# Input projection of a two-layer hybrid encoder: the last K pair of a chunk pair multiplied column by column, one more weight tile fed, heads turned in reversed order

## The chip, the cores and the metric

One NeuronCore of a Trainium2 chip. The metric is the device time of one execution of the whole program in microseconds, the median of several runs. Engine names in what follows: TensorE (PE in the profile, PEld its weight loads), VectorE (DVE), ScalarE (ACT), GpSimd (POOL), SyncE (SP), which issues nearly all transfers.

## The reference

Two layers over 256 tokens of width 2048, all in float32. Each layer mixes the tokens with 16 heads and then applies a gated feed-forward part:

```python
h = rms_norm(x, pre_mix_norm[l])
proj = h @ w_in                  # 6144 columns: q, k, v of 8 stick-breaking heads, then of 8 differential heads
o_sb = rms_norm(stick_breaking_attention(q_sb, k_sb, v_sb), sb_out_norm)
o_d  = rms_norm(differential_attention(q1, q2, k1, k2, v_d, lam), diff_subln) * (1.0 - lam_init)
x = x + rms_norm(concat(o_sb, o_d) @ w_o, post_mix_norm[l])
h = rms_norm(x, pre_ffn_norm[l])
x = x + rms_norm((silu(h @ w_gate) * (h @ w_up)) @ w_down, post_ffn_norm[l])
```

The stick-breaking heads weigh each earlier key by a sigmoid and by the cumulative product of what the keys between have left over; the differential heads subtract two softmaxes and rotate a quarter of each query and key (partial rotary).

## The kernel before, in words

**Float32 by halves.** Every operand of a big matmul is split into a rounded half `hi` and a remainder `lo`, and a product of two such operands takes three matmuls: hi by hi (L1254 in the input projection), lo of the weights (L1255), lo of the activations (L1256). The activations stand still in TensorE (128 by 128), and 512 weight columns stream past them.

**The weight stream.** All weights lie in DRAM in the order of use, which `weight_order` writes out (L119 and L120 for the plain part of the input projection), as tiles of 512 KB: 128 partitions, two K blocks, 512 columns. SyncE loads each into one of four `raw` buffers (L285), ScalarE rounds it to `hi` (L407 plain; L355, L362, L381 for mixed tiles), and VectorE subtracts to get `lo` (L346). `hi` and `lo` have six buffers each, handed round in the order of the tiles. When TensorE's program asks for a tile with `weights(i, ahead)`, the jobs of the tiles up to `ahead` further on are written into the program of ScalarE and VectorE; LOOKAHEAD = 4 (L29). A scheduler then orders each engine's instructions, and each engine works through its own list in that order.

**The input projection.** The 6144 columns are 12 chunks of 512, taken in six pairs, PAIRS = ((6, 8), (10, 7), (9, 0), (11, 2), (1, 3), (4, 5)). Chunks 0 to 5 are q, k and v of the stick-breaking heads, 6 to 11 those of the differential heads; even ones hold heads 0 to 3, odd ones heads 4 to 7. A chunk pair has four PSUM banks: two token tiles t by two columns (`col` 0 or 1). K is worked off in eight K pairs `kp`. In all but the first chunk pair some of the K pairs come first in a form of seven products in place of eight (`phased`; their tiles are mixed ones, with a `u1` tile for the parts that stay); the rest are plain (`eight_in`, L1050). In the last plain K pair `eight_in` runs for t = 0 alone, with both columns, and `settle(0)` evicts the two banks, then the same for t = 1. `settle` (L1080) copies each bank by ScalarE into a token tile `tok` (L1095) or into v (L1089), and has GpSimd rotate the differential q and k. The very first chunk pair is in `opening` (L966), without feeding ahead.

**Attention between the matmuls.** `tick()` is called throughout, and lets waiting generators issue a step. `flip` (L1099) turns a chunk's four heads by TensorE (L1113) and ScalarE (L1114); when q and k of a group are there, `stick_weights` or `diff_weights` makes the attention weights, and `attend` (L810) multiplies them with v for two heads at a time, into a bank `o` of which there is one. `attending` lets one head pair hold it; `norm_pair` (L766) takes squares (L774), scales by VectorE into `on` (L779), and lowers `attending` (L782); some ticks later TensorE turns the result into `oT_ps` (L795), and ScalarE and VectorE make the two halves of `mix` (L797, L800), which is the stationary operand of the output projection.

**The output projection** runs mixed for the K pairs 4 to 6 and plain for 7, 0, 2, 1, 3. K pair 1 needs the head pair `sb0_0_1`, its tiles are 110 and 111; K pair 3 needs the last head pair of all, `sb0_1_1`, its tiles are 112 and 113. Tiles 114 and 115 belong to the next columns and to heads that are long done; 116 and 117 are loaded into buffers V (L285) and mixed with each other (L328, L322), and before these loads stand reloads of `x` (L479) on SyncE. In layer 1 the same tiles carry numbers higher by 394, and the stage lies 1078 us later.

Of the kernel before, what the change touches and what calls it, by code (L numbers as in the profile page):

```python
# [9 lines left out]
F32 = mybir.dt.float32  # L10
F32R = mybir.dt.float32r
BF16 = mybir.dt.bfloat16
AF = mybir.ActivationFunctionType
# [4 lines left out]
P = 128  # L18
# [3 lines left out]
NT = S // P  # L22
KT = D // P
NH = 8
FF = 5632
CW = 512
# [62 lines left out]
def weight_order():  # L89
# [7 lines left out]
    def queue_pair(name, l, kp, c):  # L97
        return queue((name, l, 2 * kp, c), (name, l, 2 * kp + 1, c))
# [14 lines left out]
    for l in range(L):  # L113
        lay = {"in": {}, "o": {}, "gate": {}, "up": {}, "down": {}}
        for n, (ca, cb) in enumerate(PAIRS):
            if n:
                queue_phase(("in", l, n), "w_in", l, IN_SEVENS[n], (ca, cb))
            for kp in IN_PLAIN[n]:
                lay["in"][ca, kp] = queue_pair("w_in", l, kp, ca)  # L119
                lay["in"][cb, kp] = queue_pair("w_in", l, kp, cb)  # L120
        queue_phase(("o", l), "w_o", l, O_PHASED, (0, 1))
        order_o = [(c, kp) for kp in O_PLAIN for c in (0, 1)]
        order_o += [(c, kp) for kp in LATE_O for c in (2, 3)] + [(c, kp) for c in (2, 3) for kp in LAST_O]
# [71 lines left out]
def kernel(  # L195
# [262 lines left out]
    def weights(i, ahead):  # L458
        feed_jobs(jobs_to[i] + ahead)
        return ready[i]  # L460
# [309 lines left out]
    def norm_pair(pool, ob, mix, mixed, h0, gcol, nm):  # L770
        ss = small.tile([P, 4], F32, tag="oss", name=f"oss_{nm}")
        for i in range(4):
# [6 lines left out]
        nc.vector.tensor_tensor(  # L779
            out=on, in0=ob.rearrange("p (i d) -> p i d", i=4), in1=rs.unsqueeze(2).to_broadcast([P, 4, P]), op=ALU.mult  # L780
        )
        attending[0] -= 1  # L782
        yield
        yield
        if nm[0] == "d":
            yield
# [179 lines left out]
    def opening(pool, accs, xT, stats, sums_of, settle):  # L966
# [47 lines left out]
        for kp in range(KT // 2):  # L1014
            if kp:
                split(2 * kp)
                split(2 * kp + 1)
            if kp + 2 < KT // 2:
                load()
                fetch(2 * kp + 6)  # L1020
            for part in ((0,), (1,)) if kp == KT // 2 - 1 else (range(NT),):
                eight_in(accs, xT, 0, PAIRS[0], kp, part, kp == 0, kp == KT // 2 - 1, 0)
                if kp == KT // 2 - 1:
                    settle(part[0])
            if 3 <= kp < 7:
                next(stats)
            if 3 <= kp < 5:
                sums_of(kp - 3)
# [21 lines left out]
    def eight_in(accs, xT, l, cc, kp, toks, first, last, ahead=LOOKAHEAD):  # L1050
        ws = [weights(plan[l]["in"][c, kp], ahead) for c in cc]
        for kk in range(2):
            for t in toks:
                tick()
                st = xT[2 * kp + kk]
                stat = (st[:, 0, t * P : (t + 1) * P], st[:, 1, t * P : (t + 1) * P])
                for col, (hi, lo) in enumerate(ws):
                    product(accs[2 * t + col], stat, (hi[:, kk, :], lo[:, kk, :]), first and kk == 0, last and kk == 1)
# [8 lines left out]
    def mixer_in(pool, l, rs, xT, mix, mixed, began):  # L1067
# [7 lines left out]
        for n, cc in enumerate(PAIRS):  # L1075
# [1 line left out]
            alone = n == len(PAIRS) - 1  # L1077
            toks = {}

            def settle(t):  # L1080
                with tc.high_priority(offset=URGENT):
                    for col, c in enumerate(cc):
                        kind, g = divmod(c, 2)
                        src = banks[2 * t + col]
                        st = heads.setdefault((kind // 3, g), {"w": {}, "pT": {}, "scored": 0})
                        if kind in (2, 5):
                            if t == 0:
                                st["half"] = pool.tile([P, NT, CW], F32, tag="v", bufs=2, name=f"v{l}_{c}")
                            nc.scalar.activation(st["half"][:, t, :], src, AF.Copy, scale=rs[t][:, 0:1])  # L1089
                            if t == 1:  # L1090
                                st["v"] = st["half"]
                            continue
                        by = {0: 1, 1: 0, 3: 2, 4: 0}[kind]
                        tok = pool.tile([P, CW], F32, tag="tok", name=f"tok{l}_{c}_{t}")
                        nc.scalar.activation(tok, src, AF.Copy, scale=rs[t][:, by : by + 1])  # L1095
                        if kind in (3, 4):
                            rotate(pool, tok, t, f"{l}_{c}_{t}")
                        toks[c, t] = tok

            def flip(c, toks):  # L1100
                kind, g = divmod(c, 2)
# [27 lines left out]
            else:  # L1129
# [6 lines left out]
                for j, kp in enumerate(kps):  # L1136
# [12 lines left out]
                        rs += [inv_rms(t, pool, f"in{l}", part=began[1][t]) for t in range(NT)]  # L1149
                        scales(rs)  # L1150
                    if last:
                        for t in range(NT):
                            eight_in(banks, xT, l, cc, kp, (t,), False, last)
                            settle(t)
                    else:
                        eight_in(banks, xT, l, cc, kp, range(NT), False, last)
# [94 lines left out]
    def product(a, stat, moving, first, last):  # L1251
        sh, sl = stat
        hi, lo = moving
        nc.tensor.matmul(a, sh, hi, start=first, stop=False, skip_group_check=open_sums[0])  # L1254
        nc.tensor.matmul(a, sh, lo, start=False, stop=False, skip_group_check=open_sums[0])  # L1255
        return nc.tensor.matmul(a, sl, hi, start=False, stop=last, skip_group_check=open_sums[0])  # L1256
# [526 lines left out]
```

## Time and profile before

| | |
|---|---|
| median of 3 runs | 2170.24 us (2170.0 to 2171.7) |
| the profiled execution | 2169.97 us, its span 2168.3 us |
| TensorE busy | 2154.1 us, 99% of the span |
| VectorE, ScalarE, GpSimd busy | 1986.9, 1434.7, 241.1 us |
| input projection, layer 0 / layer 1 | up to about 299 us / 1078 to 1377 us |
| TensorE clock granted | 0.999 of full speed |

Reading it: a row of a timeline gives the start in us from the span's beginning, the duration in us, engine, line, operation, output <- inputs by the program's names, shapes and types, a count when like instructions follow one another, and in brackets how long the engine stood idle before it and for whom. A row of the windows gives the stretch, its length, busy time and count of instructions for PE, PEld, DVE, ACT and POOL, then the granted clock, the share of the DMA engines and GB/s. A row of the waits gives the engine, what it waited for, the sum in us, how often, and the longest.

### The profile page before, as it was taken

The numbers are of one execution on the slowest core, as the hardware profiler recorded it, in microseconds if no ns is written. First come the engines' busy times: TensorE is split into PE (matmuls) and PEld (weight loads), VectorE is DVE, ScalarE is ACT, GpSimd is POOL, SyncE is SP. The second block draws the span as 40 slices with busy tenths as digits, with TensorE's granted clock in tenths as the row PEclk, the third lists the DMA queues.
The fourth block names the chain that finished last, engine by engine and source line by source line (L and its number), as shares of the span: only waits on it lengthen the run. The fifth ranks groups of instructions, "written<-read, shape, count | busy, mean of one in ns | idle before, by whom it ended". The sixth has DMA issues, their size and how long they took to land.

```text
span 2168.3 us, 28898 instructions
## 1 busy us (share of the span) xinstructions
PE 2154.1 (99%) x9896; PEld 1773.9 (82%) x9896; DVE 1986.9 (92%) x2767; ACT 1434.7 (66%) x2163; POOL 241.1 (11%) x234
## 2 busy tenths in 40 slices
PE   9999999999999999999999999999999999999998
PEld 7888888888888888888878888888888888888887
DVE  7898987899999999999897989888999999999997
ACT  7667775766766666666575777757566666666664
POOL 1110000021221220000020100000112222100000
PEclk9999999999999999999999999999999999999999
DMA  8554556497887776777465555555978878767683
GB/s 295 183 193 157 173 175 246 156 309 235 243 264 224 233 240 226 227 228 253 147 207 188 176 182 175 182 204 190 308 218 269 242 224 241 230 218 245 201 270 99
DMA packets 143155, 470.43 MB, mean 217 GB/s; under 512 B 16272, under 2 KB 17296, under 8 KB 142496
## 3 DMA queue, kind: packets, MB, share of 16 engines
q1 hardware_dynamic: 124832, 436.03, 57.9%
q0 software_dynamic: 17600, 32.02, 9.0%
q8 instruction: 77, 1.26, 0.2%
q14 instruction: 70, 0.57, 0.1%
q10 hardware_dynamic: 576, 0.54, 0.1%
HBM read 460.14 MB, written 8.39 MB: 216 GB/s over the span
## 4 chain that ended last, share of the span: by engine, by line
PE 91%; DVE 4%; ACT 2%; DMA 2%; issue 1%; DVEq 0%; ACTq 0%
PE c L1311 21%; PE in L1255 5%; PE in L1254 5%; PE in L1256 5%; PE dn L1634 4%; PE dn L1631 4%; PE dn L1632 4%; PE p L1255 3%; PE p L1256 3%; PE c L1255 3%; PE c L1254 3%; PE c L1256 3%; PE p L1254 3%; DVE lo L346 2%; PE o L693 2%; PE o L695 2%
## 5 line engine op out<-in xcount | busy, mean ns | idle before, releaser
L346 DVE TENSOR_TENSOR lo<-raw,hi 128x1024 fp32r<-128x1024 f32 (+1 forms) x512 | 594.6, 1179 | 62.1 <-ACT hi L407 35.8
L407 ACT ACTIVATE hi<-raw 128x1024 fp32r<-128x1024 f32 x440 | 450.9, 1057 | 107.2 <-DMA raw<-in_weights_in_turn_dram 71.9
L1311 PE MATMUL c<-hi,xF 128*128 128x512 f32 x1344 | 364.3, 392 | 0.5 <-DVE xF L608 0.5
L1311 PEld LDWEIGHTS c<-hi,xF 128*128 128x128 f32 x1344 | 249.9, 188 | 52.6 <-DVE xF L608 1.3
L301 POOL DMA_DIRECT2D T<-in_weights_in_turn_dram x122 | 106.9, 876 | 1364.8 <-DMA T<-in_weights_in_turn_dram 279.2
L1311 PE MATMUL c<-lo,xF 128*128 128x512 f32 x672 | 207.5, 390 | 0.0
L322 ACT ACTIVATE Th<-T 128x512 fp32r<-128x512 f32 x122 | 77.2, 632 | 182.8 <-DVE T L333 180.6
L322 ACT ACTIVATE Th<-G 128x1024 fp32r<-128x1024 f32 x122 | 129.0, 1058 | 77.0 <-DVE G L334 75.8
L1631 PE MATMUL dn<-hi,jh 128*128 128x512 f32 x416 | 162.1, 390 | 0.0
L1632 PE MATMUL dn<-lo,jh 128*128 128x512 f32 x416 | 161.9, 389 | 0.0
L324 DVE TENSOR_TENSOR Tl<-G,Th 128x1024 fp32r<-128x1024 f32 x122 | 148.8, 1220 | 11.6 <-ACT Th L322 11.6
L407 ACT ACTIVATE hi<-G 128x1024 fp32r<-128x1024 f32 x122 | 129.0, 1057 | 41.6 <-DMA G<-in_weights_in_turn_dram 21.3
L324 DVE TENSOR_TENSOR lo<-T,hi 128x1024 fp32r<-128x1024 f32 x122 | 152.1, 1247 | 0.0
L334 DVE TENSOR_TENSOR G<-G,T 128x1024 f32<-128x1024 f32 x122 | 148.6, 1218 | 1.8
L1311 PEld LDWEIGHTS c<-lo,xF 128*128 128x128 f32 x672 | 126.0, 188 | 26.4
L346 DVE TENSOR_TENSOR lo<-G,hi 128x1024 fp32r<-128x1024 f32 x106 | 129.2, 1219 | 10.5 <-ACT hi L407 10.5
L322 ACT ACTIVATE hi<-T 128x1024 fp32r<-128x1024 f32 x122 | 128.1, 1050 | 12.0 <-PE c L1256 9.1
L1634 PE MATMUL dn<-hi,jl 128*128 128x512 f32 x416 | 128.2, 389 | 0.0
L1254 PE MATMUL in<-hi,xT 128*128 128x512 f32 x309 | 122.2, 398 | 0.8 <-ACT hi L1008 0.8
L1255 PE MATMUL in<-lo,xT 128*128 128x512 f32 x309 | 120.9, 392 | 1.4 <-DVE lo L346 1.4
L1256 PE MATMUL in<-hi,xT 128*128 128x512 f32 x309 | 120.3, 390 | 0.0
L1254 PE MATMUL in<-hi,xI 128*128 128x512 f32 x285 | 114.2, 401 | 0.0
(462 smaller groups left out, 5064.3 us busy)
## 6 DMA issues: line engine op xcount, KB each, us to landing
raw<-in_weights_in_turn_dram SPq DMA_DIRECT2D x510, 512.0 KB, 4.9
T<-in_weights_in_turn_dram SPq DMA_DIRECT2D x122, 512.0 KB, 5.3
G<-in_weights_in_turn_dram SPq DMA_DIRECT2D x122, 512.0 KB, 5.4
T<-in_weights_in_turn_dram POOLq DMA_DIRECT2D x122, 256.0 KB, 5.6
u<-in_weights_in_turn_dram SPq DMA_DIRECT2D x36, 256.0 KB, 5.7
V<-in_weights_in_turn_dram SPq DMA_DIRECT2D x8, 512.0 KB, 4.6
away_ffn<-x SPq DMA_DIRECT2D x8, 512.0 KB, 7.2
xd<-away_ffn SPq DMA_DIRECT2D x8, 512.0 KB, 8.7
```

What stands on the lines that cost most here:

```text
L322: nc.scalar.activation(h, w, AF.Copy)
L324: newest_rest[i] = nc.vector.tensor_tensor(out=l, in0=w, in1=h.bitcast(F32), op=ALU.subtract)
L334: nc.vector.tensor_tensor(out=g, in0=g, in1=t2.unsqueeze(1).to_broadcast([P, 2, CW]), op=ALU.add)
L346: rests.append(nc.vector.tensor_tensor(out=lo, in0=src, in1=hi.bitcast(F32), op=ALU.subtract))
L407: nc.scalar.activation(hi, raw, AF.Copy)
L1254: nc.tensor.matmul(a, sh, hi, start=first, stop=False, skip_group_check=open_sums[0])
L1255: nc.tensor.matmul(a, sh, lo, start=False, stop=False, skip_group_check=open_sums[0])
L1256: return nc.tensor.matmul(a, sl, hi, start=False, stop=last, skip_group_check=open_sums[0])
L1311: nc.tensor.matmul(a, stat[part], w[j][:, kk, :], start=first and kk + n == 0, stop=last and kk == 1 and n == 2)
L1631: nc.tensor.matmul(accs[c, t], sh, hi[:, kk, :], start=first, stop=False, skip_group_check=open_sums[0])
L1632: nc.tensor.matmul(accs[c, t], sh, lo[:, kk, :], start=False, stop=False, skip_group_check=open_sums[0])
L1634: nc.tensor.matmul(accs[c, t], sl, hi[:, kk, :], start=False, stop=last, skip_group_check=open_sums[0])
```

## The change

Four edits, all in the order of the work; the instructions of every engine stay the same in kind and number.

1. In the last plain K pair of a chunk pair, the weight stream has the tile of column 1 ahead of that of column 0.
2. The new `last_in` works that K pair column by column: column 1 for both token tiles, then column 0; after each token tile `settle(t, col)` evicts one bank. Before column 1 the stream is fed four tiles ahead, before column 0 five; in `opening` too, where nothing was fed ahead before.
3. The chunks of a pair start to be turned in reversed order, the second first.
4. `norm_pair` lowers `attending` one step later, so that a head pair holds the bank `o` for one step (two ticks) more.

```diff
@@ -116,8 +116,8 @@
             for kp in IN_PLAIN[n]:
-                lay["in"][ca, kp] = queue_pair("w_in", l, kp, ca)
-                lay["in"][cb, kp] = queue_pair("w_in", l, kp, cb)
+                for c in (cb, ca) if kp == IN_PLAIN[n][-1] else (ca, cb):
+                    lay["in"][c, kp] = queue_pair("w_in", l, kp, c)
...
@@ -779,8 +779,8 @@
+        yield
         attending[0] -= 1
-        yield
         yield
...
@@ -1018,10 +1018,10 @@
-            for part in ((0,), (1,)) if kp == KT // 2 - 1 else (range(NT),):
-                eight_in(accs, xT, 0, PAIRS[0], kp, part, kp == 0, kp == KT // 2 - 1, 0)
-                if kp == KT // 2 - 1:
-                    settle(part[0])
+            if kp == KT // 2 - 1:
+                last_in(accs, xT, 0, PAIRS[0], kp, settle)
+            else:
+                eight_in(accs, xT, 0, PAIRS[0], kp, kp == 0, 0)
...
@@ -1047,15 +1047,30 @@
+    def last_in(accs, xT, l, cc, kp, settle):
+
+        newest = plan[l]["in"][cc[0], kp]
+        ws = [weights(plan[l]["in"][c, kp], 0) for c in cc[::-1]][::-1]
+        for col in (1, 0):
+            feed_jobs(jobs_to[newest] + LOOKAHEAD + 1 - col)
+            hi, lo = ws[col]
+            for t in range(NT):
+                tick()
+                for kk in range(2):
+                    st = xT[2 * kp + kk]
+                    stat = (st[:, 0, t * P : (t + 1) * P], st[:, 1, t * P : (t + 1) * P])
+                    product(accs[2 * t + col], stat, (hi[:, kk, :], lo[:, kk, :]), False, kk == 1)
+                settle(t, col)
...
@@ -1077,25 +1092,25 @@
-            def settle(t):
+            def settle(t, col):
+                c = cc[col]
...
@@ -1149,11 +1164,9 @@
                     if last:
-                        for t in range(NT):
-                            eight_in(banks, xT, l, cc, kp, (t,), False, last)
-                            settle(t)
+                        last_in(banks, xT, l, cc, kp, settle)
...
@@ -1161,7 +1174,7 @@
             wait = 3
-            for c in cc:
+            for c in cc[::-1]:
```

(`eight_in` loses its arguments `toks` and `last`, and the rest of `settle` is unindented.)

ScalarE's program at the start of the sixth chunk pair in layer 0, before. `hi83` and `hi85` are rounded tiles of the sixth pair, `tok0_1_0` is layer 0, chunk 1, token tile 0; `a_sb` are the weights of a stick-breaking head pair in the making.

```order
L362 ACTIVATE hi83_1_2387<-raw83_2379 128x512
L1095 ACTIVATE tok0_1_0_2424<-in0_1_0_1950,rs_in0_0_494 128x512
L1095 ACTIVATE tok0_3_0_2426<-in0_3_0_1951,rs_in0_0_494 128x512
L855 ACTIVATE a_sb0_0_1_2414<-zb_sb0_0_1_2407 128x256
L797 ACTIVATE mix_df0_1_0_2428<-oT_ps_df0_1_0_2429,gains_89 128x256
L856 ACTIVATE a_sb0_0_1_2414<-a_sb0_0_1_2414 128x768
L797 ACTIVATE mix_df0_1_0_2428<-oT_ps_df0_1_0_2429,gains_89 128x256
L858 ACTIVATE a_sb0_0_1_2414<-a_sb0_0_1_2414 128x768
L1095 ACTIVATE tok0_1_1_2453<-in0_1_1_1952,rs_in0_1_508 128x512
L1095 ACTIVATE tok0_3_1_2455<-in0_3_1_1953,rs_in0_1_508 128x512
L355 ACTIVATE hi85_0_2468<-raw85_2466 128x1024
L362 ACTIVATE hi85_1_2474<-u1_84_0_2462 128x512
```

And after:

```order
L1110 ACTIVATE tok0_3_0_2398<-in0_3_0_1952,rs_in0_0_494 128x512
L918 ACTIVATE e1_df0_1_2_1_2389,sm_df0_1_2_1_2387<-s1_df0_1_2_1_2340,mx_df0_1_2_1_2345 128x256
L1110 ACTIVATE tok0_3_1_2408<-in0_3_1_1954,rs_in0_1_508 128x512
L362 ACTIVATE hi83_1_2380<-raw83_2372 128x512
L355 ACTIVATE hi85_0_2416<-raw85_2414 128x1024
L1110 ACTIVATE tok0_1_0_2428<-in0_1_0_1951,rs_in0_0_494 128x512
L1110 ACTIVATE tok0_1_1_2440<-in0_1_1_1953,rs_in0_1_508 128x512
L362 ACTIVATE hi85_1_2447<-u1_84_0_2410 128x512
L855 ACTIVATE a_sb0_0_1_2464<-za_sb0_0_1_2456 128x512
L362 ACTIVATE hi85_1_2447<-raw85_2414 128x512
L855 ACTIVATE a_sb0_0_1_2464<-zb_sb0_0_1_2457 128x256
L856 ACTIVATE a_sb0_0_1_2464<-a_sb0_0_1_2464 128x768
```

The tile `hi85_0` stood behind all four evictions and the steps of `a_sb`; now it follows `hi83_1` and the two evictions of chunk 3, with chunk 1's evictions and `a_sb` behind it.

TensorE's program in the output projection of layer 0, before; `o0_c_t` are the banks, `oT_ps_sb0_1_1` the last head pair turned.

```order
L694 MATMUL o0_1_1_2952<-lo109_3225,mix_sb0_1_0_1_3238 128x512
L695 MATMUL o0_1_1_2952<-hi109_3224,mix_sb0_1_0_1_3238 128x512
L795 MATMUL oT_ps_sb0_1_1_3387<-ident_90,on_sb0_1_1_3347 128x128 x4
L693 MATMUL o0_0_0_2949<-hi110_3262,mix_sb0_0_1_0_3328 128x512
L694 MATMUL o0_0_0_2949<-lo110_3263,mix_sb0_0_1_0_3328 128x512
L695 MATMUL o0_0_0_2949<-hi110_3262,mix_sb0_0_1_0_3328 128x512
L693 MATMUL o0_0_1_2951<-hi110_3262,mix_sb0_0_1_0_3328 128x512
```

And after:

```order
L693 MATMUL o0_1_1_2950<-hi111_3280,mix_sb0_0_1_1_3338 128x512
L694 MATMUL o0_1_1_2950<-lo111_3281,mix_sb0_0_1_1_3338 128x512
L695 MATMUL o0_1_1_2950<-hi111_3280,mix_sb0_0_1_1_3338 128x512
L795 MATMUL oT_ps_sb0_1_1_3417<-ident_90,on_sb0_1_1_3383 128x128 x4
L693 MATMUL o0_2_0_3485<-hi114_3371,mix_df0_1_0_2482 128x512
L694 MATMUL o0_2_0_3485<-lo114_3372,mix_df0_1_0_2482 128x512
L695 MATMUL o0_2_0_3485<-hi114_3371,mix_df0_1_0_2482 128x512
L693 MATMUL o0_2_1_3487<-hi114_3371,mix_df0_1_0_2482 128x512
L694 MATMUL o0_2_1_3487<-lo114_3372,mix_df0_1_0_2482 128x512
L695 MATMUL o0_2_1_3487<-hi114_3371,mix_df0_1_0_2482 128x512
L693 MATMUL o0_0_0_2947<-hi112_3308,mix_sb0_1_1_0_3415 128x512
L694 MATMUL o0_0_0_2947<-lo112_3309,mix_sb0_1_1_0_3415 128x512
```

The turning of `sb0_1_1` stood ahead of tile 110's matmuls; it now follows those of tile 111, 24 matmuls later, and six matmuls of tile 114 stand between it and the first matmul that uses `mix_sb0_1_1_0`.

ScalarE's program in the same place, before:

```order
L407 ACTIVATE hi112_3324<-raw112_3322 128x1024
L407 ACTIVATE hi113_3363<-raw113_3361 128x1024
L797 ACTIVATE mix_sb0_1_1_0_3385<-oT_ps_sb0_1_1_3387,gains_89 128x256
L407 ACTIVATE hi114_3381<-raw114_3379 128x1024
L797 ACTIVATE mix_sb0_1_1_1_3386<-oT_ps_sb0_1_1_3387,gains_89 128x256
L407 ACTIVATE hi115_3410<-raw115_3408 128x1024
L407 ACTIVATE hi116_3428<-V116_3426 128x1024
L322 ACTIVATE hi117_3452<-V117_3450 128x1024
L700 ACTIVATE jm_o0_0_0_3444,ssm_o0_0_2947<-o0_0_0_2949 128x512
```

And after:

```order
L407 ACTIVATE hi113_3333<-raw113_3331 128x1024
L576 ACTIVATE ors_sb0_1_1_3375<-rsq_sb0_1_1_3376 128x4
L797 ACTIVATE mix_sb0_0_1_1_3338<-oT_ps_sb0_0_1_3339,gains_89 128x256
L407 ACTIVATE hi114_3371<-raw114_3369 128x1024
L407 ACTIVATE hi115_3399<-raw115_3397 128x1024
L407 ACTIVATE hi116_3428<-V116_3426 128x1024
L322 ACTIVATE hi117_3452<-V117_3450 128x1024
L797 ACTIVATE mix_sb0_1_1_0_3415<-oT_ps_sb0_1_1_3417,gains_89 128x256
L797 ACTIVATE mix_sb0_1_1_1_3416<-oT_ps_sb0_1_1_3417,gains_89 128x256
L322 ACTIVATE T2h117_3456<-V117_3450 128x512
L700 ACTIVATE jm_o0_0_0_3444,ssm_o0_0_2945<-o0_0_0_2947 128x512
```

The copies `mix_sb0_1_1_0` and `_1` stood around `hi114`; they now stand behind `hi116` and `hi117`, the tiles that are made from V. Layer 1 shows the same two shifts.

More of the change, by code (lines that the diff above doesn't have):

```diff
@@ L1048, in scales, with eight_in @@
             nc.vector.tensor_scalar_mul(rs[t][:, 2:3], rs[t][:, 0:1], 1.0 / 8.0)
-    def eight_in(accs, xT, l, cc, kp, toks, first, last, ahead=LOOKAHEAD):
+    def eight_in(accs, xT, l, cc, kp, first, ahead=LOOKAHEAD):
         ws = [weights(plan[l]["in"][c, kp], ahead) for c in cc]
         for kk in range(2):
-            for t in toks:
+            for t in range(NT):
                 tick()
@@ L1057, in eight_in @@
                 for col, (hi, lo) in enumerate(ws):
-                    product(accs[2 * t + col], stat, (hi[:, kk, :], lo[:, kk, :]), first and kk == 0, last and kk == 1)
+                    product(accs[2 * t + col], stat, (hi[:, kk, :], lo[:, kk, :]), first and kk == 0, False)
+    def last_in(accs, xT, l, cc, kp, settle):
[4 more added lines that the diff above has]
+            hi, lo = ws[col]
+            for t in range(NT):
+                tick()
[4 more added lines that the diff above has]
+                settle(t, col)
     def pair_forms(pool, spool, bufs, tiles, kp, nm, **kw):
@@ L1078, in mixer_in @@
             toks = {}
-            def settle(t):
-                with tc.high_priority(offset=URGENT):
[L1082 to L1098, printed above, removed]
+            def settle(t, col):
+                c = cc[col]
+                kind, g = divmod(c, 2)
+                src = banks[2 * t + col]
+                st = heads.setdefault((kind // 3, g), {"w": {}, "pT": {}, "scored": 0})
+                with tc.high_priority(offset=URGENT):
+                    if kind in (2, 5):
+                        if t == 0:
+                            st["half"] = pool.tile([P, NT, CW], F32, tag="v", bufs=2, name=f"v{l}_{c}")
+                        nc.scalar.activation(st["half"][:, t, :], src, AF.Copy, scale=rs[t][:, 0:1])
+                        if t == 1:
+                            st["v"] = st["half"]
+                        return
+                    by = {0: 1, 1: 0, 3: 2, 4: 0}[kind]
+                    tok = pool.tile([P, CW], F32, tag="tok", name=f"tok{l}_{c}_{t}")
+                    nc.scalar.activation(tok, src, AF.Copy, scale=rs[t][:, by : by + 1])
+                    if kind in (3, 4):
+                        rotate(pool, tok, t, f"{l}_{c}_{t}")
+                    toks[c, t] = tok
             def flip(c, toks):
@@ L1151, in mixer_in @@
                     if last:
-                        for t in range(NT):
-                            eight_in(banks, xT, l, cc, kp, (t,), False, last)
-                            settle(t)
+                        last_in(banks, xT, l, cc, kp, settle)
                     else:
-                        eight_in(banks, xT, l, cc, kp, range(NT), False, last)
+                        eight_in(banks, xT, l, cc, kp, False)
                     if ahead and heads[0, 1].keys() >= {"qdone", "kdone"}:
```

## The prediction

> **What bounds the kernel now.** I began with the page: busy time per engine and the chain that ended last.
>
> ```profile
> span 2168.3 us, 28898 instructions
> PE 2154.1 (99%) x9896; PEld 1773.9 (82%) x9896; DVE 1986.9 (92%) x2767; ACT 1434.7 (66%) x2163; POOL 241.1 (11%) x234
> PE 91%; DVE 4%; ACT 2%; DMA 2%; issue 1%; DVEq 0%; ACTq 0%
> ```
>
> TensorE is the bound, busy 2154.1 of 2168.3 us, and the change takes no matmul away and adds none. So the end moves only with TensorE's waits, and these I read next, from its waits by releaser.
>
> ```profile
> PE in L1255 <- DVE lo L346: 4.0, 8, 0.7
> ```
>
> Eight times, 4.0 us in all, the second matmul of a product (L1255, on the low half `lo` of a weight tile) waits for VectorE's subtraction (L346) that makes that half. This is what the change can remove. TensorE's timeline shows where; six of the eight waits lie in two places per layer: where the sixth chunk pair begins (252 and 255 us, in layer 1 at 1330 and 1333), and where the fourth does (154 and 1233).
>
> ```profile
> 250.93 0.39 PE L1256 MATMUL in<-hi,xT 128*128 128x512 f32 x1
> 251.16 0.40 PE L1254 MATMUL in<-hi,xT 128*128 128x512 f32 x1
> 252.30 0.50 PE L1255 MATMUL in<-lo,xT 128*128 128x512 f32 x1 [0.74 <-DVE lo L346]
> ...
> 254.98 0.50 PE L1255 MATMUL in<-lo,shin 128*128 128x512 f32 x1 [0.56 <-DVE lo L346]
> ...
> 1330.38 0.50 PE L1255 MATMUL in<-lo,xI 128*128 128x512 f32 x1 [0.38 <-DVE lo L346]
> ...
> 1333.05 0.50 PE L1255 MATMUL in<-lo,shin 128*128 128x512 f32 x1 [0.56 <-DVE lo L346]
> ...
> 154.23 0.50 PE L1255 MATMUL in<-lo,shin 128*128 128x512 f32 x1 [0.55 <-DVE lo L346]
> ...
> 1232.75 0.50 PE L1255 MATMUL in<-lo,shin 128*128 128x512 f32 x1 [0.54 <-DVE lo L346]
> ```
>
> Undisturbed matmuls start 0.23 us apart (250.93 to 251.16). The waiting one starts 1.14 after its forerunner (251.16 to 252.30): 0.91 lost, of which the bracket shows 0.74. The other 0.17 is TensorE's pipeline filling again, so every such wait costs its bracket and 0.17: 0.91 + 0.73 in layer 0 and 0.55 + 0.73 in layer 1 at the sixth pair, 2.92 us; 0.72 + 0.71 at the fourth, 1.43 us.
>
> Why is `lo` late at the sixth pair? VectorE's timeline there, then ScalarE's.
>
> ```profile
> 244.76 0.48 DVE L800 SCALAR_TENSOR_TENSOR mix_df<-oT_ps_df,gains,mix_df 128x256 fp32r<-128x256 f32 x1 [0.69 <-ACT mix_df L797]
> 245.85 0.48 DVE L800 SCALAR_TENSOR_TENSOR mix_df<-oT_ps_df,gains,mix_df 128x256 fp32r<-128x256 f32 x1 [0.61 <-ACT mix_df L797]
> 246.58 0.69 DVE L860 SCALAR_TENSOR_TENSOR a_sb<-za_sb,a_sb 128x512 f32<-128x512 f32 x1 [0.25 <-ACT a_sb L858]
> ...
> 248.69 1.22 DVE L346 TENSOR_TENSOR lo<-raw,hi 128x1024 fp32r<-128x1024 f32 x1 [1.08 <-ACT hi L355]
> ```
>
> ```profile
> 242.30 0.63 ACT L362 ACTIVATE hi<-raw 128x512 fp32r<-128x512 f32 x1 [1.63 <-DVE raw L360]
> ...
> 246.42 1.29 ACT L1095 ACTIVATE tok<-in,rs_in 128x512 f32<-128x512 f32 x2
> 247.56 1.09 ACT L355 ACTIVATE hi<-raw 128x1024 fp32r<-128x1024 f32 x1
> ```
>
> VectorE stands idle 0.69 + 0.61 + 0.25 + 1.08 = 2.63 us in front of the late subtractions, and the last of these waits is for `hi` (L355, tile 85), which ScalarE makes at 247.56, behind two evictions (L1095) that need the end of the fifth pair. The weights themselves are long there.
>
> ```profile
> 224.80 35.15 SPq L285 DMA_DIRECT2D raw<-in_weights_in_turn_dram  x8
> ```
>
> The group's first two loads (224.80 and the next) are tiles 85 and 86, over 20 us before their use: a queue order and a feeding limit, not a transfer, hold them.
>
> **The change part by part.** *Column by column, and a fifth tile fed.* In ScalarE's new order `hi85_0` stands right behind the second half of `hi83_1`, the row at 242.30, and no longer behind the exponentials and all four evictions. Its buffer is that of tile 79 (six rotate), and 79 is now used up by the first half of the last plain pair. So it can start near 242.9 instead of 247.56, and VectorE's 2.63 us of idle time can fill. The two waits need `lo` 0.91 + 0.73 = 1.64 us earlier, counting that TensorE itself comes earlier after the first; 2.63 covers that with 1.0 to spare, and layer 1 asks for less (1.28). Bounds: nothing gained, if `hi86` (its buffer is tile 82's, first used by the sixth pair itself) holds the second `lo`; all 2.92 at best. I take **-2.92**, because the buffer of 82_0 is free after that pair's first six matmuls, which is before `lo` of 86 is wanted. At the fourth pair it is another matter:
>
> ```profile
> 138.00:154.00 16.00, 15.68 (x73) 12.42 (x71) 15.81 (x30) 12.96 (x26) 7.24 (x8) 1.00 0.20 71
> ```
>
> VectorE (the third of the busy times) works 15.81 of the 16 us before that wait. An earlier `hi` does little for an engine without idle time; I take 0 there, and -1.43 as the bound. The two waits left of the eight, 0.67 of brackets (4.0 less the 3.33 of the six rows), lie at the start and in the second pair; I take 0 for them too. Evicting by column costs nothing: no row of TensorE's waits names an eviction (L1095, L1089), and the four are as many as before. On SyncE the two `u` loads of the sixth pair (`u1_81`) go ahead of five loads of 512 KB:
>
> ```profile
> raw<-in_weights_in_turn_dram SPq DMA_DIRECT2D x510, 512.0 KB, 4.9
> ```
>
> The 20 us of lead above cover that; without it a tile would land late by up to these 4.9 us. GpSimd, 11% busy, turns the heads of column 8 before those of column 6, two jobs of one length.
>
> *Heads turned in reversed order, a pair attending one tick longer.* No row of the waits names the bank `o`, so the longer hold by itself is worth 0. But both push the last stick-breaking head pair, `sb0_1_1`, back, and this meets the output projection, where order decides. In the new order TensorE's transposes of that pair (L795) come 24 matmuls later, six matmuls ahead of the first use of their result, and ScalarE copies the result (L797) behind `hi116` and `hi117`, which are made from V, the last loads of the queue. Before:
>
> ```profile
> 342.91 1.06 ACT L407 ACTIVATE hi<-V 128x1024 fp32r<-128x1024 f32 x1 [1.55 <-DMA V<-in_weights_in_turn_dram]
> 346.00 1.06 ACT L322 ACTIVATE hi<-V 128x1024 fp32r<-128x1024 f32 x1 [2.03 <-DVE V L328]
> 346.96 0.58 ACT L700 ACTIVATE jm_o<-o 128x512 f32<-128x512 f32 x1
> ```
>
> ```profile
> 336.17 0.47 ACT L797 ACTIVATE mix_sb<-oT_ps_sb,gains 128x256 fp32r<-128x256 f32 x1
> ```
>
> ```profile
> 341.44 0.39 PE L693 MATMUL o<-hi,mix_sb 128*128 128x512 f32 x1
> ...
> 342.80 0.39 PE L693 MATMUL o<-hi,mix_sb 128*128 128x512 f32 x1
> ```
>
> The copy was made at 336.17 and first used at 341.44. Now six matmuls of `hi114` stand in between, so TensorE wants it at 342.80; ScalarE is free of `hi117` at 346.96 and takes 0.47: 347.43. By these times TensorE would wait 4.6 us; queued behind the copy on ScalarE are the second copy and the squares (L700), and behind the waiting matmul all of TensorE. In layer 1 V comes sooner:
>
> ```profile
> 1420.87 0.39 PE L693 MATMUL o<-hi,mix_sb 128*128 128x512 f32 x1
> ```
> ```profile
> 1422.12 0.58 ACT L700 ACTIVATE jm_o<-o 128x512 f32<-128x512 f32 x1
> ```
>
> There it is 1422.12 + 0.47 - 1420.87 = 1.7 us. These are upper ends, since V may land earlier. Its load follows the `x` reloads on SyncE, which wait for VectorE, and the transfers have nothing to do before them:
>
> ```profile
> 314.42 2.69 SPq L479 DMA_DIRECT2D x<-in_x_dram  x4
> ```
> ```profile
> 310.00:314.00 4.00, 4.00 (x21) 3.41 (x22) 4.00 (x6) 2.34 (x3) 0.00 (x0) 1.00 0.01 2
> ```
> ```profile
> 299.04 1.23 DVE L346 TENSOR_TENSOR lo<-raw,hi 128x1024 fp32r<-128x1024 f32 x1 [2.60 <-ACT hi L355]
> ...
> 1377.11 1.23 DVE L346 TENSOR_TENSOR lo<-raw,hi 128x1024 fp32r<-128x1024 f32 x1 [2.93 <-ACT hi L355]
> ```
>
> DMA share 0.01 from 310 to 314. VectorE stood idle 2.60 us (2.93) at the end of the sixth pair, again for a `hi` behind evictions, which the fifth tile moves ahead of them; from there to the reloads it has no gap. If that fills, the reloads, and V behind them, come as much sooner against TensorE: 4.6 - 2.6 = 2.0 us left in layer 0, 1.7 - 2.9 below zero, so 0, in layer 1. The ends are 0 and 6.3 for both; I take **+2.0**, the reading of the rows just quoted.
>
> Sum: -2.92 + 2.0 = -0.9 against the profiled execution (2169.97 us: span 2168.3 and 1.7 around it), 2169.1. The median of the runs, 2170.24, is 0.27 above it; by the median I say **2169.3 us**. About 0.2% of it, 4.3 us, is what a measurement can tell from no change.
>
> **The rivals.** *Faster:* V lands early enough that the output projection has no wait, and the waits at the fourth pair go too, since the tile order there moves as well: -2.92 - 1.43 = -4.35, 2165.9 us. For it speaks the empty DMA stretch, against it VectorE's 15.81 of 16 us.
>
> *Slower:* the copies wait for V as before's times have it, because VectorE spends the freed 2.6 us on other queued work and the reloads start no sooner against TensorE; and only the first wait in each layer's sixth pair goes (0.91 + 0.55 = 1.46). Then 4.6 + 1.7 - 1.46 = +4.8, 2175.1 us. V's `hi` decides it: if both layers come d sooner, the loss is 4.6 + 1.7 - 2d, which equals the 2.92 gained at d = 1.7, V's `hi` at 341.2 instead of 342.91 by the old clock; later than that the change costs time. Against it speaks the 0.01.
>
> *Slower, with the clock:* a wait that long could also cost TensorE its clock. At the program's end, TensorE's last two matmuls and the windows after them read:
>
> ```profile
> 2162.09 1.12 PE L746 MATMUL xb_d<-mg_d,r_d 128*128 128x512 f32 x2 [1.72 <-ACT r_d L745]
> ```
> ```profile
> 2164.00:2165.00 1.00, 0.00 (x0) 0.00 (x0) 0.00 (x0) 0.00 (x0) 0.00 (x0) 1.00 1.07 329
> 2165.00:2166.00 1.00, 0.00 (x0) 0.00 (x0) 0.00 (x0) 0.00 (x0) 0.00 (x0) 0.52 1.07 351
> ```
>
> The last work ends at 2162.09 + 1.12 = 2163.2; the granted clock (the third figure from the right) is 1.00 until 2165 and 0.52 after, some 1.8 us later. A 4.6 us wait is longer than that. How long the clock then takes to return no row shows; if as long as the wait itself, 2.3 us are lost (4.6 us at half speed): 2177.4 us. The Trainium skill, "TensorE: Matmul & The Clock Gate", section "What's actually happening", states that the clock halves after an idle window of about 3.4 us and is given back after about 3.4 us of work; by it the loss is an estimated 1.7 us instead, and a 2.0 us wait would leave the clock alone, which the fall after some 1.8 us here does not bear out clearly, since other short idle stretches stand before it.
>
> *No relief:* the sixth pair's waits stay, since `hi86` waits for tile 82's buffer, and the +2.0 comes: 2172.2 us, within the bound.
>
> **How the numbers follow.** Forecast 0.50; faster rival 0.20, of which half reaches past 4.3 us; no relief 0.12; slower 0.13; with the clock 0.05. So faster by over 0.2%: 0.10; slower: 0.18; the rest, 0.72, within. The range leaves out the two slow cases (0.18) and reaches from 2165.5, the faster rival with 0.4 for a wait or two more, to 2174.0, the no-relief case with 1.8 more in the output projection.
>
> **What would show it.** Right: no wait on `lo` near 251 and 253 us, nor 1078 us later; `hi` of tile 85 near 243; one TensorE wait of about 2 us on `mix_sb` (L797) near 341 in layer 0 and under 0.3 in layer 1; the `x` reloads 2 to 4 us earlier. Wrong: waits on `lo` that only moved; V at its old time; a TensorE wait at a place named nowhere above, or a granted clock under 1.00 near 341.

## The result and the profile after

| | before | after |
|---|---|---|
| median | 2170.08 us (16 runs, 2168.87 to 2171.7) | 2174.82 us (16 runs, 2172.12 to 2179.36) |
| ratio | | 1.0024 [1.0017, 1.0030] |
| profiled execution | 2169.97 us, span 2168.3 | 2173.02 us, span 2171.3 |

The change costs 4.7 us, outside the predicted range, and the runs of the new order also spread wider. The page of after, in the same places as that of before:

```profile
span 2171.3 us, 28885 instructions
PE 2153.4 (99%) x9896; PEld 1773.5 (82%) x9896; DVE 1991.4 (92%) x2767; ACT 1436.6 (66%) x2163; POOL 242.8 (11%) x234
PE 83%; DVE 9%; DMA 3%; ACT 3%; issue 2%; DVEq 0%; SPq 0%; ACTq 0%
```

The busy times have hardly moved, so the loss lies in waits. The chain that ended last runs 83% through TensorE where it was 91%, and 9% through VectorE where it was 4%. TensorE's waits, by releaser:

```profile
PE in L1268 <- DVE lo L346: 3.6, 6, 1.1
PE xb_d L746 <- ACT r_d L745: 1.7, 1, 1.7
PE o_sb L824 <- ACT v L1104: 1.5, 2, 0.9
PE in L1267 <- ACT hi L1008: 1.4, 1, 1.4
PE spare L513 <- DVE idle L510: 1.3, 1, 1.3
PE o_sb L824 <- DVE on_sb L779: 0.9, 1, 0.9
PE qkT_ps L1128 <- ACT kT L1129: 0.9, 2, 0.4
```

(L1267, L1268 and L1269 of after are L1254, L1255 and L1256 of before; L1104 and L1110 are `settle`, L1128 and L1129 `flip`.) The waits on `lo` are 3.6 us where they were 4.0, and three rows are new: on v (1.5), on the scaled head pair `on_sb`, whose bank `o` is the only one (0.9), and on turned heads `kT` (0.9). At the sixth pair one wait is left in each layer, longer than either of the two before; here is layer 0's:

```profile
253.91 0.39 PE L1267 MATMUL in<-hi,shin 128*128 128x512 f32 x1
255.41 0.50 PE L1268 MATMUL in<-lo,shin 128*128 128x512 f32 x1 [1.12 <-DVE lo L346]
```

Two bracketed waits of 0.74 and 0.56 have become one of 1.12; in layer 1, 0.38 and 0.56 one of 0.81. ScalarE shows that the edit did what it says:

```profile
244.39 0.63 ACT L362 ACTIVATE hi<-raw 128x512 fp32r<-128x512 f32 x1
244.93 1.04 ACT L355 ACTIVATE hi<-raw 128x1024 fp32r<-128x1024 f32 x1
```

`hi85` comes at 244.93, not 247.56. But VectorE's gaps did not fill with `lo` alone. Its timeline after:

```profile
246.33 1.22 DVE L346 TENSOR_TENSOR lo<-raw,hi 128x1024 fp32r<-128x1024 f32 x1
247.47 0.35 DVE L929 TENSOR_SCALAR e_df<-e_df,sm_df 128x256 f32<-128x256 f32 x1
247.73 0.69 DVE L360 TENSOR_TENSOR raw<-raw,u 128x512 f32<-128x512 f32 x1
248.33 0.69 DVE L346 TENSOR_TENSOR lo<-u,hi 128x512 fp32r<-128x512 f32 x1
248.93 0.48 DVE L930 SCALAR_TENSOR_TENSOR e_df<-e_df,sm_df,e_df 128x256 f32<-128x256 f32 x1
...
254.68 0.68 DVE L346 TENSOR_TENSOR lo<-u,hi 128x512 fp32r<-128x512 f32 x1
```

L929 and L930 end the softmaxes of a differential head pair. They stand between the subtractions now, and the `lo` at 254.68 ends (255.36) just when the waiting matmul starts (255.41). In before the same softmax was over long before:

```profile
237.92 0.61 DVE L929 TENSOR_SCALAR e_df<-e_df,sm_df 128x256 f32<-128x256 f32 x2
```

The windows give the sum for 13 us around the start of the sixth pair, VectorE being the third busy time; before, then after:

```profile
242.00:255.00 13.00, 11.69 (x53) 8.89 (x51) 10.37 (x17) 12.70 (x21) 0.00 (x0) 1.00 0.21 68
```
```profile
242.00:255.00 13.00, 12.29 (x60) 9.97 (x58) 13.00 (x24) 12.65 (x24) 0.00 (x0) 1.00 0.22 81
```

VectorE was busy 10.37 of 13 us, and is now busy all 13.00.

Single waits vary between executions by some tenths, so the waits of three traces of each kernel were added up (before: the shown one and two more below; after likewise; both layers, brackets in us, mean of the three):

| TensorE waits for | before | after |
|---|---|---|
| `lo`, fourth pair | 1.01 | 1.79 |
| `lo`, sixth pair | 2.33 | 2.05 |
| `kT`, turned heads | 0 | 0.90 |
| v | 0 | 1.35 |
| bank `o` (`on_sb`) | 0 | 0.63 |
| `mix_sb`, output projection | 0 | 0.79 |
| sum | 3.34 | 7.51 |

That is 4.2 us more, and with about four more waits at the prediction's 0.17 of refilling each some 4.8, against 4.7 timed (the three executions traced differ by 4.4 us in the mean). All of TensorE's waits together are 9.5 us in before and 14.3 in after, so the rows left out of the table add some 0.6; they differ by more than that between traces of one kernel (4.8 to 8.1 us in before).

### The profile page after: what moved, and what is told of

Read it like the earlier page. It is cut to its first block, busy times and chain, and to the rows that moved or that the text cites. A ratio compares the mean times of both kernels' runs of the same rounds, so it can differ in the third digit from the quotient of the medians.

```text
span 2171.3 us, 28885 instructions
## 1 busy us (share of the span) xinstructions
PE 2153.4 (99%) x9896; PEld 1773.5 (82%) x9896; DVE 1991.4 (92%) x2767; ACT 1436.6 (66%) x2163; POOL 242.8 (11%) x234
## 4 chain that ended last, share of the span: by engine, by line
PE 83%; DVE 9%; DMA 3%; ACT 3%; issue 2%; DVEq 0%; SPq 0%; ACTq 0%
PE c L1324 21%; DVE lo L346 5%; PE dn L1645 4%; PE dn L1644 4%; PE dn L1647 4%; PE in L1268 4%; PE in L1269 3%; PE in L1267 3%; DMA raw<-in_weights_in_turn_dram 3%; PE p L1268 3%; PE p L1269 3%; PE c L1269 3%; PE c L1268 3%; PE p L1267 3%; PE c L1267 3%; PE o L693 2%
## 5 line engine op out<-in xcount | busy, mean ns | idle before, releaser
L1267 PE MATMUL in<-hi,xT 128*128 128x512 f32 x309 | 122.4, 398 | 1.4 <-ACT hi L1008 1.4
L1268 PE MATMUL in<-lo,xT 128*128 128x512 f32 x309 | 120.7, 391 | 0.9 <-DVE lo L346 0.7
L1269 PE MATMUL in<-hi,xT 128*128 128x512 f32 x309 | 120.5, 390 | 0.0
L1267 PE MATMUL in<-hi,xI 128*128 128x512 f32 x285 | 113.9, 400 | 0.0
```

## The experiments

Two theories stood against each other at first: that the longer hold (edit 4) makes the loss, by way of the bank `o` and the copies behind V; and that the new order at the pairs' ends (edits 1 to 3) makes it, and the hold nothing. Each ratio below is to before timed beside the experiment on the same chip, where before's median was 2172.5 to 2173.3 us; times from different chips compare by these ratios alone. The brackets are 95% intervals, and a run without a ratio is a single execution.

**The change again, and each part alone.** The first is after unchanged:

> The changed kernel once more, for a second trace of it. Both theories: +3 to +6 us on the kernel before. Theory A (the output projection carries the loss, by copies that stand behind the last loads): in a slower run than the one traced, TensorE waits longer for mix_sb there, 1 us or more. Theory B (the loss is many small waits that the column order and the hold make: for v, for the bank o, for kT): the waits on v (0.5 and 0.9 us), on the bank o (0.9) and on lo of the sixth pair (1.1 and 0.8) are there again within 0.3 us each, and the wait for mix_sb stays under 0.3.

Measured 2177.65 us, 1.0022 [1.0013, 1.0030]: the loss repeats, and so do the waits on v (0.8 us), on the bank `o` (0.7) and on `kT` (0.9). In this trace the output projection of layer 1 has a wait on `mix_sb` as well. ScalarE and TensorE there:

```profile
1425.20 1.06 ACT L322 ACTIVATE hi<-V 128x1024 fp32r<-128x1024 f32 x1 [2.36 <-DVE V L328]
1426.17 0.46 ACT L797 ACTIVATE mix_sb<-oT_ps_sb,gains 128x256 fp32r<-128x256 f32 x1
...
1426.68 0.50 PE L693 MATMUL o<-hi,mix_sb 128*128 128x512 f32 x1 [1.19 <-ACT mix_sb L797]
```

The copy stands behind a tile made from V, as predicted, but it is the second one, which waits 2.36 us for VectorE's mixing (L328), and it is in layer 1.

The hold alone, on the kernel before:

```diff
-        attending[0] -= 1
         yield
+        attending[0] -= 1
```

> The kernel before with edit 4 alone: a head pair attends one step longer. Theory A: the loss sits here, since the transposes of the last head pair move 24 matmuls later and one copy stands between the two V tiles: +1.5 to +4 us, with a wait on mix_sb of 1 us or more in layer 0. Theory B: only the wait on the bank o comes, under +1.5 us. The sixth pair's waits on lo stay at 0.7 and 0.6 by both.

Measured 2175.83 us, 1.0017 [1.0008, 1.0026]. Its waits show no row for the bank `o`; they show the copies:

```profile
PE in L1255 <- DVE lo L346: 3.5, 7, 0.6
...
PE o L693 <- ACT mix_sb L797: 1.5, 2, 1.3
```

The columns alone (edits 1 and 2 on the kernel before):

> The kernel before with edits 1 and 2 alone: the last plain pair column by column, the fifth tile fed. Theory A: a gain of 1 to 3 us, since the sixth pair's waits on lo go and nothing is lost later. Theory B: no gain, 0 to +3 us, with waits on v before the output projection (0.5 to 0.9 us in each layer).

Measured 2175.63 us, 1.0015 [1.0006, 1.0024]. The turning alone:

```diff
-            for c in cc:
+            for c in cc[::-1]:
```

> The kernel before with edit 3 alone: the chunks turned in reversed order. Both theories give within 1 us of before; the copies of the last head pair stay ahead of V here. More than +2 us would mean that the turning order itself carries the loss, which neither says.

Measured 2176.76 us, 1.0019 [1.0010, 1.0028]. Each of these two brings a wait that neither before nor after has. TensorE's waits of the columns alone, then of the turning alone:

```profile
PE qkT_ps L1128 <- POOL tok L964: 1.5, 1, 1.5
```
```profile
PE qkT_ps L1113 <- POOL tok L964: 1.6, 1, 1.6
```

L964 ends GpSimd's rotation of a differential chunk, in the first chunk pair, at 60 us. By the order, each edit alone has a chunk turned first whose banks are not the first evicted; both together restore that. So edits 1 and 3 belong together, and their single times don't add up to the whole. Neither theory had this wait.

**The change without the hold** (edits 1 to 3):

```diff
-        yield
         attending[0] -= 1
+        yield
         yield
```

> The changed kernel without edit 4: columns, fifth tile and reversed turning stay. Theory A (the longer hold carries the loss, by the copies of the last head pair behind V): 2 to 4 us faster than the changed kernel, so between -1 and +1.5 us on the kernel before, and no wait on mix_sb. Theory B (many small waits of the column order): +2.5 us or more, with the waits on v, on kT and on lo of the sixth pair as in the changed kernel.

Measured 2175.49 us, 1.0013 [1.0004, 1.0022]. Both theories get a part: without the hold the loss is 1.0013 where after has 1.0024 and 1.0022 (the intervals overlap), and the rows for the bank `o` and `mix_sb` are gone, those on v and `kT` not:

```profile
PE in L1268 <- DVE lo L346: 2.3, 5, 1.1
...
PE o_sb L824 <- ACT v L1104: 1.2, 2, 0.9
PE qkT_ps L1128 <- ACT kT L1129: 0.9, 2, 0.4
```

**Which part of edits 1 to 3?** Four edits of that kernel. Four tiles fed in place of five:

```diff
-            feed_jobs(jobs_to[newest] + LOOKAHEAD + 1 - col)
+            feed_jobs(jobs_to[newest] + LOOKAHEAD)
```

> Edits 1 and 3 without the hold and without the fifth tile: four tiles ahead before both columns. If the fifth tile gains what the prediction said (the sixth pair's waits on lo), this is 1 to 3 us slower than the kernel without the hold alone. If VectorE has no room for it, it is within 0.7 us of that.

Measured 2175.78 us, 1.0011 [1.0002, 1.0020]: the fifth tile is worth nothing that can be measured. A run of before beside it:

> The kernel before once more, for a second trace of it: waits on lo at the fourth and sixth pair within 0.2 us of the first trace, none on mix_sb, v or the bank o. Where its clock runs later than in the first trace though the program is the same, that part of any difference is no effect of an edit.

Measured 2172.25 us. The waits on `lo` at the fourth and sixth pair come to 3.4 us, where the first trace had 3.3, but single ones differ by up to 0.37. And one new row shows a matmul at the end of the fifth pair that waits for an eviction, which the first trace, the one that the prediction went by, did not have:

```profile
247.91 0.50 PE L1254 MATMUL in<-hi,shin 128*128 128x512 f32 x1 [0.38 <-ACT tok L1095]
```

Then the order of the last pair, whose two chunks are both v, reversed: chunk 4, the v of heads 0 to 3, becomes column 1 and is evicted first.

```diff
-PAIRS = ((6, 8), (10, 7), (9, 0), (11, 2), (1, 3), (4, 5))
+PAIRS = ((6, 8), (10, 7), (9, 0), (11, 2), (1, 3), (5, 4))
```

> The kernel without the hold, and the last pair taken as (5, 4) in place of (4, 5), so that v of the heads that attend first is evicted with the first column. Theory B: the wait for v before the output projection goes, 0.4 to 1.1 us per layer, so 0.8 to 2 us faster than without this. Theory A: under 0.8 us of effect.

Measured 2175.15 us, 1.0012 [1.0003, 1.0021]. The waits on v are gone, and this row stands in their place:

```profile
PE o_sb L824 <- DVE on_sb L779: 1.1, 2, 0.8
```

The head pair that no longer waits for v waits for the bank of the one before it: the time is that of the kernel without the hold. Before against itself, to see what the method tells apart:

> The kernel before against itself, timed as the others were. It shows what the timing makes of no change: within 0.7 us by every theory. If it came out 1.5 us or more slower, that much of every figure above would belong to the timing.

Measured 2171.37 us, 0.9997 [0.9988, 1.0006]. The ratio shows no difference, but the two medians are 1.2 us apart (2172.54 beside it): 1 us between two medians is not yet an effect.

**Copies ahead of V.** After, with tile 116 rounded only behind the two copies, and V fed two tiles later:

```diff
-            nc.scalar.activation(hi, raw, AF.Copy)
+            rounded = nc.scalar.activation(hi, raw, AF.Copy)
+            if i + 1 in own:
+                tc.add_manual_dep(rounded.ins, newest_copy[0].ins.name, AFTER, reason="the copies first")
...
```

> The changed kernel with one thing undone: in the output projection the V tile 116 is rounded only behind the two copies of the last head pair (and V is fed two tiles later). The longer hold stays, and the transposes stay 24 matmuls late. Theory A (copies behind V): the wait on mix_sb falls from about 1.2 us to under 0.6, and 1 to 2.5 us of the changed kernel's loss go. If the hold costs by something else, the time stays within 0.7 us of the changed kernel.

Measured 2176.55 us, 1.0020 [1.0011, 1.0029]. The wait on `mix_sb` is gone, and the time is that of after on the same chip:

> The changed kernel a third time, on the same chip as the three others, for direct comparison: +4 to +5.5 us on the kernel before; the waits on mix_sb between 0 and 1.5 us.

Measured 2176.55 us, 1.0023 [1.0013, 1.0033]. So taking this wait away gains nothing that can be told: by what was expected, the hold costs by something else in this kernel. The one trace has a wait of 0.56 us for `x` at 1469 us that no other trace has; where the rest of the 1.2 us went stays open.

**The turning in the third pair.** The kernel without the hold, with the third and the last pair listed in reverse, so that the reversed turning takes chunk 9, a differential one, first again, as before did:

```diff
-PAIRS = ((6, 8), (10, 7), (9, 0), (11, 2), (1, 3), (4, 5))
+PAIRS = ((6, 8), (10, 7), (0, 9), (11, 2), (1, 3), (5, 4))
```

> Without the hold, and two pairs with their columns exchanged: (0, 9) for (9, 0), so that the chunk that GpSimd rotates is evicted with the first column, and (5, 4) for (4, 5). If the fourth pair's wait on lo (1.15 us at 154 us without the hold) comes from the rotation running late beside VectorE, it falls under 0.7, and the whole is 0.5 to 1.5 us faster than without the hold alone (+2.5). If not, that wait stays and so does the time.

Measured 2174.49 us, 1.0012 [1.0003, 1.0020]. The fourth pair's waits, for which it was made, did not fall (0.92 and 1.62 us). But the softmax is early again, and the sixth pair's waits are 0.26 and 0.41. VectorE:

```profile
240.07 0.61 DVE L929 TENSOR_SCALAR e_df<-e_df,sm_df 128x256 f32<-128x256 f32 x2
```

The traces with the column order at the fifth pair, or the new turning, fall into two groups by the first such row. In the five with an early softmax (237 to 241 us: the columns alone, this one, and three below that change the fifth pair only) no layer's sixth pair waits more than 0.42 us in all. In the ten with a late one (244 to 248 us) every layer waits 0.81 us or more, save both layers of one trace (0.25 and 0.48, the kernel without the hold) and layer 0 of another (no wait, the copies ahead of V). The turning alone is one of the ten; VectorE and TensorE:

```profile
247.93 0.35 DVE L929 TENSOR_SCALAR e_df<-e_df,sm_df 128x256 f32<-128x256 f32 x1
...
258.72 0.50 PE L1255 MATMUL in<-lo,shin 128*128 128x512 f32 x1 [1.26 <-DVE lo L346]
```

The softmax is late in every trace that turns chunk 0 ahead of chunk 9, with edits 1 and 2 or without, and in no other. So edit 3 pushes it into the place that edits 1 and 2 clear.

**The fifth pair alone.** Before, with the column order and the fifth tile at the end of the fifth pair only, turning and hold as before:

```diff
+                for c in (cb, ca) if n == 4 and kp == IN_PLAIN[n][-1] else (ca, cb):
...
+                    if last and n == 4:
+                        last_in(banks, xT, l, cc, kp, settle)
```

> The kernel before, with the column order and the fifth tile in one place only, the end of the fifth chunk pair (1, 3); turning order and hold as before. If the prediction's term was right in itself, the sixth pair's waits on lo fall from 1.3 and 1.0 us to under 0.4 each and the time by 1.5 to 2.9 us, since the output projection keeps its order. If VectorE has no room there, the waits stay over 0.8 and the time within 0.7 us of before.

Measured 2172.03 us, 0.9992 [0.9984, 1.0001]. Its waits on `lo`, the window that held 10.37 and 13.00 us of VectorE's work, and what is left of the sixth pair's waits in layer 0:

```profile
PE in L1274 <- DVE lo L346: 1.7, 5, 0.6
...
242.00:255.00 13.00, 12.75 (x58) 9.91 (x57) 11.43 (x18) 12.63 (x21) 0.00 (x0) 1.00 0.25 82
...
252.89 0.50 PE L1274 MATMUL in<-lo,shin 128*128 128x512 f32 x1 [0.16 <-DVE lo L346]
```

`lo` costs 1.7 us where it cost 4.0, and VectorE is busy 11.43 of the 13: the mechanism of the forecast, in a kernel where nothing else moves into the gap. Timed again on another chip:

> The kernel with the column order at the end of the fifth pair alone, timed a second time. If the gain is real: 1 to 3 us faster than before, ratio 0.9986 to 0.9995, and the sixth pair's waits on lo under 0.4 us each again. If the first timing was chance: a ratio of 0.9997 or more.

Measured 2172.27 us, 0.9994 [0.9985, 1.0003]. The sixth pair's waits are 0.41 and 0.42 us here, just above the 0.4 expected. Both medians are 1 us below before's, but each interval reaches 1, and before against itself came out as far below: that this version is faster is not shown. The complement, the change without the hold in all pairs but the fifth (`n != 4` in the same places, `cc[::-1] if n != 4 else cc`):

> Columns, fifth tile and reversed turning in all pairs but the fifth, no longer hold. If the loss that stays without the hold comes from these pairs (waits on v, on kT, on lo of the fourth pair), this is 2 to 4 us slower than before. If it came from the fifth pair's end, it is within 1 us of before.

Measured 2174.8 us, 1.0006 [0.9997, 1.0015], 1.8 us above before and between the two cases expected. There is no wait for v in it, 1.1 us on `kT` and 2.3 at the sixth pair. And the kernel without the hold again beside it:

> The changed kernel without the hold, for a second trace: by the first, waits of 0.45 on kT and 0.3 to 0.9 on v per layer, 1.15 on lo of the fourth pair in layer 0, 0.25 and 0.48 at the sixth. If the timed loss of 2.5 us is made of waits, this trace shows 1 to 2 us more of them than the first.

Measured 2176.65 us, 3.3 us above the execution of the first trace. The rows of the table above sum to 5.4 us in it and to 4.0 in the first: 1.4 more, as expected if the loss is made of waits, and most of it at the sixth pair (2.6 us, the first had 0.7). By the medians the fifth pair alone gains 1 us, the others alone lose 1.8, and together they lose 2.4; only the last is clear of no change. That the gain is lost beside the others rests on the sixth pair's waits more than on these times. Last, the fifth pair alone with the hold:

> As the kernel with the fifth pair alone, with the longer hold added. If the hold acts only in the output projection (copies between the two V tiles), it costs 1.5 to 3 us there with a wait on mix_sb of about 1.3, and the sixth pair's waits stay as without it. If it also pushes VectorE's attention work into the sixth pair's start, those waits are back at 0.8 or more and the cost is 3 us or more.

Measured 2175.57 us, 1.0011 [1.0003, 1.0020], 3.5 us above the same kernel without it on the same chip. The sixth pair has no wait in either layer. The one large new row is that of the copies, and layer 0 shows the predicted chain whole:

```profile
PE o L693 <- ACT mix_sb L797: 2.4, 2, 1.8
...
342.62 1.06 ACT L407 ACTIVATE hi<-V 128x1024 fp32r<-128x1024 f32 x1 [1.09 <-DMA V<-in_weights_in_turn_dram]
343.58 0.46 ACT L797 ACTIVATE mix_sb<-oT_ps_sb,gains 128x256 fp32r<-128x256 f32 x1
...
344.09 0.50 PE L693 MATMUL o<-hi,mix_sb 128*128 128x512 f32 x1 [1.75 <-ACT mix_sb L797]
```

V lands, its tile is rounded, the copy follows, TensorE starts. That a kernel which is early here pays the hold in full, and one that has lost time before pays less, since it reaches V later, fits these rows, but was not tried by itself.

## Why the prediction was wrong

The bound was read rightly: the work of every engine stayed, and the time moved with TensorE's waits. Two steps of the sum failed outright, and two held only in part.

*"2.63 covers that with 1.0 to spare", -2.92.* `hi85` came earlier as said (244.93 us, not yet 242.9), and the first wait of each layer's sixth pair went. But the idle time was counted as if VectorE's other work stayed where it was. In after the softmax of the differential head pair, which edit 3 sends later, fills it: the sixth pair's waits fell by 0.28 us of brackets in the mean, not by 2.33. Where that softmax stays early, in the fifth pair alone, 0.53 and 0.83 are left of 2.33 in its two traces. The mechanism was right for that edit, and the step that failed is that the three edits were priced one by one.

*"Evicting by column costs nothing: no row of TensorE's waits names an eviction."* This left out the largest part of the loss. Rows of before show what was last to come in the old order, and the new one changes who comes last. In the columns alone the sixth pair's waits fall to 0.41 us, and yet the kernel is slower: GpSimd's rotation (1.5 us), the `lo` of the fourth pair (2.77, before 1.01) and the bank `o` (1.1) are waited for in their place. In after v costs 1.35 us. With chunk 4 evicted first that wait is gone, so the order of the evictions makes it, but not by itself: the columns alone do not have it, nor does the version with all pairs but the fifth.

The 0.90 us on `kT` go with edit 3, whose turning the sum priced at nothing as well. Every trace that turns chunk 0 ahead of chunk 9 has this wait, save the one with four tiles, and no other trace has it. The turning alone:

```profile
PE qkT_ps L1113 <- ACT kT L1114: 0.6, 1, 0.6
```

The `lo` of the fourth pair, taken as unchanged, costs 0.78 more in after. It is largest where the columns come with the old turning of the third pair (2.77 us in the columns alone, 2.54 with chunk 9 first), and 1.06 in the turning alone, so the turning is not its cause; what is, stays open.

*"The longer hold by itself is worth 0."* By itself it is, for the bank `o`: with the hold alone nobody waits for it. But in after 0.63 us are waited for it, near 322 us in layer 0, in each of the three traces. The kernel without the hold has no such wait in its two, so it takes the hold and the other edits together, and the sum priced them apart. (The columns alone, and chunk 4 evicted first, wait 1.1 us for the bank without the hold, in layer 0 before 309 us.) The copies are the next step.

*Copies behind V, "+2.0" in layer 0 and "0" in layer 1.* The order was read rightly, the size by layer was not. V's first tile of after in layer 0 and the copy, then the first matmul that uses the copy and its forerunner:

```profile
341.09 1.06 ACT L407 ACTIVATE hi<-V 128x1024 fp32r<-128x1024 f32 x1 [0.76 <-PE o L695]
...
345.06 0.46 ACT L797 ACTIVATE mix_sb<-oT_ps_sb,gains 128x256 fp32r<-128x256 f32 x1
...
345.21 0.40 PE L695 MATMUL o<-hi,mix_df 128*128 128x512 f32 x1
345.56 0.51 PE L693 MATMUL o<-hi,mix_sb 128*128 128x512 f32 x1
```

V was there: its tile waited for a buffer that TensorE still read. And TensorE itself reached the place some 2.6 us later than 342.80: it started 0.35 us after its forerunner, 0.12 more than usual, just as the copy ended (345.52). So nearly nothing was waited for here. In layer 1 the wait was 0, 1.19 and 1.19 us in the three traces. The `x` reloads did not come 2 to 4 us sooner against the old clock (314.25, before 314.42).

The measured time is that of the slower rival, 2175.1, but only a small part of it came by that rival's way (0.79 of 4.2 us of waits): that the two numbers agree is chance. The rival with the clock did not happen in after (granted clock 0.999), though it did in two experiments, below.

What the runs leave: the hold costs some 2 us on top of the other edits, as after against the kernel without it has it (the intervals overlap), 2.6 on before and 3.5 on the fifth pair alone. In the last two the copies carry it: 1.5 and 2.4 us of waits on `mix_sb`, the latter with a fall of the clock, below. In after that is not shown, since putting the copies first gained nothing. The rest, some 2.4 us, is in part the new waits at the pairs' ends, less what the sixth pair gains: the table's rows sum to 4.0 and 5.4 us in the two traces without the hold, and to 3.3 in before. What remains has no row.

## What to carry to other kernels

An idle stretch in front of a late operation is worth its length only while nothing else moves into it: of each further edit ask which queued work it sends there. A wait that the profile does not show has an unknown slack, not no cost; an edit that changes which of several results comes last must be priced by its new last one. Order edits that look like one (what is evicted first, what is turned first, which weights come first) belong together, and the fewest places that remove the wait, here one pair of six, beat the same rule applied everywhere.

## What the runs showed of the hardware

TensorE's clock can fall after a wait much shorter than the 4.6 us feared in the prediction. In the fifth pair with the hold, behind the 1.75 us wait that ends at 344.09 us (granted clock: third figure from the right):

```profile
343.00:344.00 1.00, 0.00 (x0) 0.00 (x0) 0.29 (x1) 1.00 (x2) 0.00 (x0) 1.00 1.04 426
...
345.00:346.00 1.00, 0.91 (x4) 0.41 (x3) 1.00 (x3) 0.48 (x1) 0.00 (x0) 0.90 0.98 389
346.00:347.00 1.00, 1.00 (x4) 0.81 (x4) 0.35 (x1) 0.99 (x1) 0.00 (x0) 0.50 0.96 381
347.00:348.00 1.00, 1.00 (x4) 0.81 (x3) 0.90 (x1) 0.47 (x2) 0.00 (x0) 0.50 0.29 115
...
349.00:350.00 1.00, 1.00 (x5) 0.81 (x4) 0.41 (x2) 0.56 (x2) 0.00 (x0) 0.89 0.05 20
350.00:351.00 1.00, 1.00 (x6) 0.80 (x6) 0.96 (x3) 0.00 (x0) 0.00 (x0) 1.00 0.00 0
```

And its matmuls in that stretch:

```profile
346.50 0.63 PE L694 MATMUL o<-lo,mix_sb 128*128 128x512 f32 x1
346.93 0.63 PE L695 MATMUL o<-hi,mix_sb 128*128 128x512 f32 x1
```

They start 0.43 us apart, not 0.23. The clock stood at half from about 345.8 to 349.2 us, which costs an estimated 1.7 us (half of 3.4), as much again as the wait. The same followed the 1.60 us wait at 60 us of the turning alone, from about 60.5 to 63.9 us. No wait of 1.54 us or less had this after it in any trace, up to 2155 us, nor had one of 1.62 in another (the fourth pair, layer 1, of the kernel with the third pair's turning): these runs give no sharp bound. The Trainium skill, "TensorE: Matmul & The Clock Gate", section "What's actually happening", states an idle window of about 3.4 us before the clock halves and about 3.4 us of work before it returns. The half-speed stretch of some 3.4 us agrees; the idle time does not, and here the measurement decides: 1.6 to 1.75 us were enough.
